# A latent-attention layer: element-wise work moved to GpSimd, one head group projected at a time

## The chip, the cores and the metric

The kernel runs on one core of one Trainium2 chip. The metric is the device time of one execution in microseconds (us). The engines are named as in the profile: PE is TensorE (matrix products; PEld are its weight loads), DVE is VectorE, ACT is ScalarE, POOL is GpSimd, and SP issues transfers. A line such as L922 is line 922 of the kernel before.

## The reference

The model is a trunk of two layers over 512 tokens of width 1024, in float32. Layer 0 mixes a state-space scan with gated linear attention, layer 1 is multi-head latent attention, and a SwiGLU block follows each. Only layer 1's attention is touched by the change:

```python
cq, ckv, k_rope = jnp.split(h @ w_dqkv, [MLA_Q_RANK, MLA_Q_RANK + MLA_KV_RANK], axis=-1)
q = (rms_norm(cq, q_lora_norm) @ w_uq).reshape(bsz, seqlen, H, MLA_NOPE + MLA_ROPE)
q_nope, q_rope = jnp.split(q, [MLA_NOPE], axis=-1)
kv = (rms_norm(ckv, kv_lora_norm) @ w_ukv).reshape(bsz, seqlen, H, MLA_NOPE + MLA_V)
k_nope, v = jnp.split(kv, [MLA_NOPE], axis=-1)
q_nope = rms_norm(q_nope, q_nope_norm)
q_rope = apply_rope(rms_norm(q_rope, q_rope_norm), cos[:, None, :], sin[:, None, :])
k_nope = rms_norm(k_nope, k_nope_norm)
k_rope = apply_rope(rms_norm(k_rope, k_rope_norm), cos, sin)
...
s = jnp.einsum('bqhd,bkhd->bhqk', qn, k_nope) + jnp.einsum('bqhr,bkr->bhqk', qr, k_rope)
p = jax.nn.softmax(jnp.where(mask, s * scale, -jnp.inf), axis=-1)
o = jnp.einsum('bhqk,bkhv->bqhv', p, v)
```

There are 16 heads; queries and keys have 64 plain and 32 rotary components, values 64, and the rotary key is shared by all heads. The low ranks are 384 for queries and 256 for keys and values.

## The kernel before, in words

Every large product is made in three passes of a rounded 32-bit type: each operand is split in a rounded part (hi) and the rest (lo), and hi x hi, hi x lo and lo x hi are added in one accumulator (mm3, L149 to L152). Weights come from memory through `weight` (L130): SP loads a raw tile (two buffers), ACT rounds it (L144), DVE takes the rest (L145); the rounded and the rest tiles have three buffers each. `weight` gives its instructions a priority some 90 instructions ahead, so weights are loaded as soon as a buffer comes free.

The kernel is written in program order, and a scheduler turns that order into one fixed queue per engine when the program is built: of the instructions that are ready it takes the one that stands earliest. So work that stands later in the code fills the gaps of work that stands earlier, when its inputs and buffers are there. On the chip each queue runs strictly in order.

The attention layer, in program order before the change:

1. The shared rotary key: 16 matmuls of 96 columns (L747, L748).
2. The low-rank queries (3 tiles) and keys/values (2 tiles) with their norms (L754 to L781).
3. The rotary key is turned, normalised and rotated, and copied into four key tiles kT, one by ACT (L818) and three by POOL (L820).
4. `project(0)` and `project(1)` (L957). A `project(g)` makes queries, keys and values of four heads for all 512 tokens: 36 matmuls of 384 columns and 24 of 512, evacuated by ACT (L838, L851, L852). Then squares on ACT (L856, L859), their sums on DVE (L857 to L860), an inverse root by three Newton steps on DVE (L862, L165 to L170), and on DVE the scale of the plain query part (L865), the scale of the rotary part (L868), its rotation in four steps (`rope`, L790 to L793) and the scale of the keys (L872). The query and key tiles have two buffers each, values three.
5. Eight times for a pair of heads: `prepare` of the pair after it, then `attend` of the pair itself. `prepare` transposes keys (L879) and queries (L892) on PE and evacuates them with ACT (L886, L894) and DVE (L888). `attend` goes through four blocks b of 128 queries with n = 128 (b + 1) keys. For each of the two heads j: the scores on PE (L911, two banks `sco`), scale, mask and maximum in one DVE step out of PSUM (L914), the exponent with its sum on ACT (L916); then for both heads the reciprocal (L919), the scale of the probabilities (L922, both on DVE), their transposes on PE (L925, two banks `ptr`) and the copy into `pt` by ACT (L929). The score tiles `sc` in SBUF have four buffers. At the end the values of both heads are gathered on PE (L934, bank `po`) and split into hi and lo (L126, L127).
6. `project(2)` stands behind attend 0 and `project(3)` behind attend 2 (`PROJ = (0, 2)`), the first half of the output projection (`o_round(0)`, L944) behind attend 4, the second half (`o_round(1)`) behind attend 7, and then the second SwiGLU block.

POOL is used in this layer for the mask and for the three copies of kT only.

Of the kernel before, what the change touches and what calls it, by code (L numbers as in the profile page):

```python
# [29 lines left out]
PROJ = (0, 2)  # L30
# [16 lines left out]
def kernel(ctx: ExitStack, tc: tile.TileContext, A, yT, stop=99):  # L47
# [15 lines left out]
    def acc():  # L63
        return pacc.tile([P, T], F32, tag="acc", name=nm("acc"))
# [65 lines left out]
    def weight(src, kc, m):  # L130

        with tc.high_priority(offset=AHEAD):
            return weight_now(src, kc, m)

    def weight_now(src, kc, m):
# [3 lines left out]
        return parts(r, kc, m)  # L139

    def parts(r, kc, m):
        hi = wp.tile([P, KD * P], F32R, tag="whi", name=nm("whi"))
        lo = wp.tile([P, KD * P], F32R, tag="wlo", name=nm("wlo"))
        S.copy(hi[:, :kc * m], r)  # L144
# [568 lines left out]
    with tc.tile_pool(name="mla", bufs=2) as mp, tc.tile_pool(name="mla1", bufs=1) as m1:  # L713
# [22 lines left out]
        wkr = wp.tile([P, KD * P], F32, tag="wraw", name="wkr", bufs=2)  # L736
        wkr = wkr[:, :KD * 32].rearrange("p (k m) -> p k m", k=KD)
        nc.sync.dma_start(wkr, A["w_kr"])
        w3 = wp.tile([P, KD * P], F32R, tag="whi", name="w3")
        w3 = w3[:, :KD * 96].rearrange("p (k j m) -> p k j m", k=KD, j=3)  # L740
        for j in range(2):
            S.copy(w3[:, :, j, :], wkr)
        V.tensor_tensor(w3[:, :, 2, :], wkr, w3[:, :, 0, :].bitcast(F32), ALU.subtract)
        ps = acc()
        for k, (xh, xl) in enumerate(xp):
            wk = w3[:, k].rearrange("p j m -> p (j m)")
            E.matmul(ps[:96], wk, xh, start=(k == 0), stop=False)  # L747
            E.matmul(ps[:96], wk, xl, start=False, stop=(k == KD - 1))  # L748
        krr = m1.tile([32, T], F32, name="krr")
        S.copy(krr, ps[64:96])  # L750
        V.tensor_tensor(krr, ps[:32], krr, ALU.add)

# [31 lines left out]
        def rope(dst, src, tab, shape):  # L784
# [9 lines left out]

        ps = aux()
# [26 lines left out]

        scale = 96 ** -0.5
        oparts = []

        def project(g):


            qs = mp.tile([P, 4, 4, 96], F32, tag="qs", name=nm("qs"))
            wqs = [weight(A["w_uq"][g, :, k0:k0 + n], n, 384) for k0, n in ((0, 2), (2, 1))]  # L830
            for i in range(4):
                ps = acc()
                for k in range(3):
                    lh, ll = lora["q"][k]
                    wh, wl = wqs[k // 2]
                    mm3(ps[:, :384], lh[:, i * P:(i + 1) * P], ll[:, i * P:(i + 1) * P],
                        wh[:, k % 2, :], wl[:, k % 2, :], k == 0, k == 2)
                S.activation(qs[:, i].rearrange("p h d -> p (h d)"), ps[:, :384], AF.Copy,  # L838
                             scale=cf["q"][:, i:i + 1])

            wkv = weight(A["w_ukv"][g], 2, 512)
            ks = mp.tile([P, 4, 4, 64], F32, tag="ks", name=nm("ks"))
            v = mp.tile([P, 4, 4, 64], F32, tag="v", name=nm("v"), bufs=3)
            for i in range(4):
                ps = acc()
                for k in range(2):
                    lh, ll = lora["kv"][k]
                    mm3(ps, lh[:, i * P:(i + 1) * P], ll[:, i * P:(i + 1) * P],
                        wkv[0][:, k, :], wkv[1][:, k, :], k == 0, k == 1)
                p3 = ps.rearrange("p (w h d) -> p w h d", w=2, h=4)  # L850
                S.activation(ks[:, i], p3[:, 0], AF.Copy, scale=cf["kv"][:, i:i + 1])  # L851
                S.activation(v[:, i], p3[:, 1], AF.Copy, scale=cf["kv"][:, i:i + 1])  # L852

            sq = mp.tile([P, 16, 96], F32, tag="sq", name=nm("sq"), bufs=1)
            st = mp.tile([P, 3, 16], F32, tag="st", name=nm("st"))
            S.activation(sq, qs.rearrange("p i h d -> p (i h) d"), AF.Square)  # L856
            V.tensor_reduce(st[:, 0], sq[:, :, 0:64], AX.X, ALU.add)  # L857
            V.tensor_reduce(st[:, 1], sq[:, :, 64:96], AX.X, ALU.add)
            S.activation(sq[:, :, 0:64], ks.rearrange("p i h d -> p (i h) d"), AF.Square)  # L859
            V.tensor_reduce(st[:, 2], sq[:, :, 0:64], AX.X, ALU.add)  # L860
            for j, n in enumerate((64, 32, 64)):
                V.tensor_scalar(st[:, j], st[:, j], 1.0 / n, EPS, ALU.mult, ALU.add)  # L862
            rf = rsqrt(mp, st, [P, 3, 16], "hr")
            q2 = qs.rearrange("p i h d -> p (i h) d")
            V.tensor_tensor(q2[:, :, 0:64], q2[:, :, 0:64],  # L865
                            rf[:, 0].unsqueeze(2).to_broadcast([P, 16, 64]), ALU.mult)
            rr = mp.tile([P, 16, 32], F32, tag="rr", name=nm("rr"), bufs=1)
            V.tensor_tensor(rr, q2[:, :, 64:96],  # L868
# [90 lines left out]
        for p in range(8):  # L959
# [5 lines left out]
            if p in PROJ:  # L965
                pr[2 + PROJ.index(p)] = project(2 + PROJ.index(p))
# [91 lines left out]
```

## Time and profile before

| what | value |
|---|---|
| time of three runs | 1370.97, 1372.99, 1373.26 us (median 1372.99) |
| the profiled execution's own time | 1371.09 us |
| its span, first to last instruction | 1368.9 us |
| granted TensorE clock | 0.999 |
| attention layer | from about 776 us (rotary key, L747) to about 989 us (last values, L934) |

Times in the profile are counted from the start of the span. A row of a group gives line, engine, operation, out<-in, count, then busy time and mean of one in ns, then the idle time of the engine just before these instructions and what ended it. A row of the order of time gives start and duration; several instructions can be merged in one row (x4). The rows by stretches give the busy time of each engine with the number of instructions in brackets, then the granted clock, the share of the transfer engines and GB/s. Matmul ends are modelled, so two matmuls in a row overlap in the rows.

### The profile page before, as it was taken

What the parts mean: (1) busy time and instruction counts of PE and PEld (TensorE: products, weight loads), DVE (VectorE), ACT (ScalarE), POOL (GpSimd) and SP (SyncE); (2) the same over time, 40 slices, a digit from 0 to 9 for tenths busy, and PEclk for the clock granted to TensorE, in tenths of its full rate; (3) what the DMA queues carried; (4) which work ended last, traced back from release to release, by engine and by line L of the source; (5) the groups of instructions that cost most, each with busy time, mean ns of one, the idle gap of its engine ahead of it and who ended that gap; (6) DMA issues with size and microseconds to landing.
All of it is one profiled execution on the core that took longest, in us unless ns stands there. A gap on an engine that the chain in (4) does not pass through costs nothing.

```text
span 1368.9 us, 16667 instructions
## 1 busy us (share of the span) xinstructions
PE 1344.9 (98%) x6506; PEld 1088.7 (80%) x6506; DVE 815.5 (60%) x1369; ACT 562.8 (41%) x941; POOL 7.8 (1%) x35
## 2 busy tenths in 40 slices
PE   8999999999999999999999999999999999999998
PEld 5788889788888888888888887666588888888887
DVE  7987976788867444444333469776594444443221
ACT  5584633544344322332232348775653322322121
POOL 0000000000000000000000000000000000000000
PEclk9999999999999999999999999999999999999999
DMA  5342232222233333223333321111033223323331
GB/s 177 109 141 91 77 95 78 78 77 62 79 93 105 93 94 106 92 92 99 90 100 100 101 68 56 39 47 62 1 98 103 93 93 102 98 93 108 111 103 63
DMA packets 36781, 122.22 MB, mean 89 GB/s; under 512 B 4768, under 2 KB 5792, under 8 KB 36704
## 3 DMA queue, kind: packets, MB, share of 16 engines
q1 hardware_dynamic: 35888, 120.72, 28.1%
q8 instruction: 51, 0.84, 0.2%
q10 hardware_dynamic: 816, 0.46, 0.1%
q14 instruction: 26, 0.21, 0.0%
HBM read 119.03 MB, written 2.13 MB: 89 GB/s over the span
## 4 chain that ended last, share of the span: by engine, by line
PE 90%; DVE 5%; ACT 3%; issue 1%; DMA 1%; SPq 0%; ACTq 0%
PE acc L150 27%; PE acc L151 27%; PE acc L152 27%; PE sco L911 2%; PE ptr L925 1%; PE po L934 1%; DVE wlo L145 1%; PE a L447 1%; PE a L625 0%; PE a L433 0%; PE a L614 0%; PE a L451 0%; ACT whi L144 0%; PE a L627 0%; DVE gm L534 0%
## 5 line engine op out<-in xcount | busy, mean ns | idle before, releaser
L150 PE MATMUL acc<-xh,whi 128*128 128x512 f32 x1144 | 449.1, 393 | 5.2 <-DVE dp L322 2.5
L144 ACT CAST whi<-wraw 128x1024 fp32r<-128x1024 f32 (+2 forms) x221 | 225.8, 1022 | 554.0 <-PE acc L151 436.9
L151 PE MATMUL acc<-xl,whi 128*128 128x512 f32 x1144 | 448.7, 392 | 0.0
L152 PE MATMUL acc<-xh,wlo 128*128 128x512 f32 x1144 | 448.7, 392 | 0.0
L145 DVE TENSOR_TENSOR wlo<-wraw,whi 128x1024 fp32r<-128x1024 f32 (+2 forms) x221 | 261.9, 1185 | 163.2 <-ACT whi L144 163.1
L150 PEld LDWEIGHTS acc<-xh,whi 128*128 128x128 f32 x1144 | 214.9, 188 | 51.2 <-ACT cvt L366 2.8
L152 PEld LDWEIGHTS acc<-xh,wlo 128*128 128x128 f32 x1144 | 215.1, 188 | 44.8 <-DVE wlo L145 0.6
L151 PEld LDWEIGHTS acc<-xl,whi 128*128 128x128 f32 x1144 | 215.1, 188 | 44.5 <-issue 1.4
L152 PE MATMUL acc<-fhh,wlo 128*128 128x512 f32 x288 | 112.0, 389 | 0.0
L150 PE MATMUL acc<-fhh,whi 128*128 128x512 f32 x288 | 112.0, 389 | 0.0
L151 PE MATMUL acc<-fhl,whi 128*128 128x512 f32 x288 | 112.0, 389 | 0.0
L683 DVE TENSOR_TENSOR fu<-acc,R 128x512 f32<-128x512 f32 x44 | 30.4, 691 | 136.2 <-PE acc L152 136.2
L680 DVE TENSOR_TENSOR fg<-acc,R 128x512 f32<-128x512 f32 x44 | 30.4, 691 | 89.0 <-PE acc L152 88.9
L152 PEld LDWEIGHTS acc<-fhh,wlo 128*128 128x128 f32 x288 | 54.1, 188 | 11.3
L151 PEld LDWEIGHTS acc<-fhl,whi 128*128 128x128 f32 x288 | 54.1, 188 | 11.3
L150 PEld LDWEIGHTS acc<-fhh,whi 128*128 128x128 f32 x288 | 54.1, 188 | 11.1
L151 PE MATMUL acc<-mxl,whi 128*128 128x512 f32 x128 | 49.9, 391 | 0.0
L150 PE MATMUL acc<-mxh,whi 128*128 128x512 f32 x128 | 49.8, 391 | 0.0
L152 PE MATMUL acc<-mxh,wlo 128*128 128x512 f32 x128 | 49.7, 390 | 0.0
L911 PE MATMUL sco<-kT,qT 96*128 96x128 f32 (+3 forms) x128 | 42.8, 445 | 1.5 <-DVE mx L914 1.3
L914 DVE CUSTOM_DVE_ANT_0 sc<-sco,am 128x128 f32<-128x128 f32 (+3 forms) x64 | 30.7, 487 | 13.6 <-PE sco L911 11.5
L916 ACT ACTIVATE sc<-sc,mx 128x128 f32<-128x128 f32 (+3 forms) x64 | 35.7, 561 | 7.3 <-DVE mx L914 6.8
(329 smaller groups left out, 1584.8 us busy)
## 6 DMA issues: line engine op xcount, KB each, us to landing
wraw<-in_w_gate_dram SPq DMA_DIRECT2D x44, 512.0 KB, 3.5
wraw<-in_w_up_dram SPq DMA_DIRECT2D x44, 512.0 KB, 3.5
wraw<-in_w_down_dram SPq DMA_DIRECT2D x32, 512.0 KB, 3.6
wraw<-in_w_out_dram SPq DMA_DIRECT2D x16, 512.0 KB, 3.6
wraw<-in_w_xbc_dram SPq DMA_DIRECT2D x12, 512.0 KB, 3.6
wraw<-in_w_down_dram SPq DMA_DIRECT2D x16, 384.0 KB, 3.1
wraw<-in_w_z_dram SPq DMA_DIRECT2D x8, 512.0 KB, 3.5
wraw<-in_w_v_dram SPq DMA_DIRECT2D x8, 512.0 KB, 3.5
```

Of the source, the lines that this page charges most:

```text
L144: S.copy(hi[:, :kc * m], r)
L145: V.tensor_tensor(lo[:, :kc * m], r, hi.bitcast(F32)[:, :kc * m], ALU.subtract)
L150: E.matmul(out, ah, bh, start=first, stop=False)
L151: E.matmul(out, ah, bl, start=False, stop=False)
L152: E.matmul(out, al, bh, start=False, stop=last)
L447: E.matmul(pd[64 * h:64 * h + 64, c * P:(c + 1) * P], xdt[:, c, h, :], mt[:, h, c, :], start=True, stop=True)
L680: V.tensor_tensor(g, pg, R, ALU.mult)
L683: V.tensor_tensor(u, pu, R, ALU.mult)
L911: E.matmul(ps[:, :n], qts[j][:, b * P:(b + 1) * P], kts[j][:, :n], start=True, stop=True)
L914: V.tensor_tensor_reduce(sc[:, :n], ps[:, :n], am[:, T - n:], -scale, 3e38, ALU.add, ALU.min, mx[:, j:j + 1])
L916: S.activation(sc[:, :n], sc[:, :n], AF.Exp, bias=mx[:, j:j + 1], scale=-1.0, accum_out=sm[:, j:j + 1])
L925: E.transpose(ps[:, kb * P:(kb + 1) * P], sc[:, kb * P:(kb + 1) * P], ident)
```

## The change: what it does

- `weight` and `parts` take an optional engine for the rounding; the weights of `project` and `o_round` are rounded by POOL in place of ACT (11 in the stretch of the attends, 20 in all).
- In `project`, POOL does the two scales of the queries, the rotation of the queries (`rope` takes an engine) and the scale of the keys: seven instructions for each of four groups, before on DVE.
- In `attend`, POOL scales the probabilities, before on DVE (64 instructions). The copy of the transposed probabilities is made by DVE for the second head of a pair and stays on ACT for the first.
- The order in the code: `project(0)` stands ahead of the rotary key's matmuls, which before stood ahead of the low-rank products. `project(1)`, `project(2)` and `project(3)` stand behind attends 0, 1 and 3 (`PROJ = (0, 1, 3)`).

```diff
-PROJ = (0, 2)
+PROJ = (0, 1, 3)
...
-    def parts(r, kc, m):
+    def parts(r, kc, m, copy=None):
...
-        S.copy(hi[:, :kc * m], r)
+        (copy or S.copy)(hi[:, :kc * m], r)
...
-        def rope(dst, src, tab, shape):
+        def rope(dst, src, tab, shape, V=V):
...
-            wqs = [weight(A["w_uq"][g, :, k0:k0 + n], n, 384) for k0, n in ((0, 2), (2, 1))]
+            wqs = [weight(A["w_uq"][g, :, k0:k0 + n], n, 384, G.tensor_copy) for k0, n in ((0, 2), (2, 1))]
...
-            wkv = weight(A["w_ukv"][g], 2, 512)
+            wkv = weight(A["w_ukv"][g], 2, 512, G.tensor_copy)
...
-            V.tensor_tensor(q2[:, :, 0:64], q2[:, :, 0:64],
+            G.tensor_tensor(q2[:, :, 0:64], q2[:, :, 0:64],
                             rf[:, 0].unsqueeze(2).to_broadcast([P, 16, 64]), ALU.mult)
...
-            V.tensor_tensor(rr, q2[:, :, 64:96],
+            G.tensor_tensor(rr, q2[:, :, 64:96],
                             rf[:, 1].unsqueeze(2).to_broadcast([P, 16, 32]), ALU.mult)
-            rope(qs[:, :, :, 64:96], rr.rearrange("p (i h) d -> p i h d", i=4), tabs[0], [P, 4, 4, 32])
+            rope(qs[:, :, :, 64:96], rr.rearrange("p (i h) d -> p i h d", i=4), tabs[0], [P, 4, 4, 32], G)
             k2 = ks.rearrange("p i h d -> p (i h) d")
-            V.tensor_tensor(k2, k2, rf[:, 2].unsqueeze(2).to_broadcast([P, 16, 64]), ALU.mult)
+            G.tensor_tensor(k2, k2, rf[:, 2].unsqueeze(2).to_broadcast([P, 16, 64]), ALU.mult)
...
-                    V.tensor_scalar(sc[:, :n], sc[:, :n], sm[:, j:j + 1], None, ALU.mult)
+                    G.tensor_scalar(sc[:, :n], sc[:, :n], sm[:, j:j + 1], 1.0, ALU.mult, ALU.mult)
...
-                    last = S.copy(dst, ps[:, :n].rearrange("p (k q) -> p k q", q=P))
+                    last = (V.tensor_copy if j else S.copy)(dst, ps[:, :n].rearrange("p (k q) -> p k q", q=P))
...
-                w = weight(A["w_o"][r, m2], 4, 256)
+                w = weight(A["w_o"][r, m2], 4, 256, G.tensor_copy)
...
-        pr = {0: project(0), 1: project(1)}
+        pr = {0: first}
...
-                pr[2 + PROJ.index(p)] = project(2 + PROJ.index(p))
+                pr[1 + PROJ.index(p)] = project(1 + PROJ.index(p))
```

In the code, `first = project(0)` now stands right behind the low-rank products, and the block that loads, multiplies and adds the rotary key (L736 to L751) follows it.

More of the change, by code (lines that the diff above doesn't have):

```diff
@@ L732 @@
                         pattern=[[-1, P]], channel_multiplier=1)
[L736 to L751, printed above, removed]
         lora, cf = {}, {}
```

105 lines of the change are left out of this document (61 added, 44 removed).

## The prediction

> **What bounds the kernel now.** I read the page first, then the busy time of each engine by stretches of the attention stage, then what every idle piece waited for, then the order of time on VectorE (DVE) and TensorE (PE) in the two worst places. The page:
>
> ```profile
> span 1368.9 us, 16667 instructions
> PE 1344.9 (98%) x6506; PEld 1088.7 (80%) x6506; DVE 815.5 (60%) x1369; ACT 562.8 (41%) x941; POOL 7.8 (1%) x35
> ```
>
> PE sets the time, POOL is empty. The whole kernel can't gain more than what PE loses, so the question is where PE loses time and whether the moved work causes it. By stretches (columns: PE, PEld, DVE, ACT, POOL busy, clock, DMA share, GB/s), with the last row the whole of the attends:
>
> ```profile
> 822.00:836.00 14.00, 13.49 (x71) 11.65 (x69) 13.31 (x35) 11.24 (x21) 1.75 (x3) 1.00 0.07 20
> 836.00:923.00 87.00, 78.80 (x418) 55.28 (x420) 70.50 (x214) 67.71 (x163) 0.00 (x0) 1.00 0.16 50
> 950.00:965.00 15.00, 13.88 (x77) 9.05 (x78) 11.77 (x45) 12.81 (x38) 0.00 (x0) 1.00 0.13 36
> 965.00:977.00 12.00, 11.87 (x64) 6.93 (x62) 8.32 (x33) 9.00 (x28) 0.00 (x0) 1.00 0.01 2
> 836.00:989.00 153.00, 142.91 (x751) 97.88 (x751) 110.25 (x332) 106.70 (x266) 0.00 (x0) 1.00 0.13 43
> ```
>
> From 836 to 989 us PE idles 153.00 - 142.91 = 10.1 us, and 8.2 us of that (87.00 - 78.80) lie before 923 us, where the normalisation of the projected heads shares DVE with the softmax. One attend without that, 965 to 977 us, idles 0.13 us. So the loss belongs to the projections' company, not to the attend as such. The clock is 1.00 throughout and the transfers use 13%, so neither counts. The idle time understates the loss: a matmul of 512 columns lasts 0.39 us but the next starts 0.23 us after it (the rows at 775.96 and 776.19 below), so each stop also costs some 0.16 us of overlap. Who makes PE stop, in the same stretch (total us, times, longest):
>
> ```profile
> PEld sco L911 <- DVE mx L914: 9.8, 23, 0.7
> PEld acc L150 <- ACT qT L894: 4.0, 2, 2.2
> PEld ptr L925 <- ACT pt L929: 3.0, 8, 0.5
> PEld ptr L925 <- DVE sc L922: 2.0, 4, 1.1
> ```
>
> These are 37 stops. DVE frees the score banks late (L914), ACT frees the accumulators and the transpose banks late (L894, L929). One of the worst places, on DVE and on PE:
>
> ```profile
> 870.57 1.22 DVE L865 TENSOR_TENSOR qs<-qs,hry 128x1024 f32<-128x1024 f32 x1
> ...
> 874.11 0.68 DVE L792 TENSOR_TENSOR qs<-rr,csq 128x512 f32<-128x512 f32 x1
> 874.71 0.55 DVE L914 CUSTOM_DVE_ANT_0 sc<-sco,am 128x384 f32<-128x384 f32 x1
> ...
> 870.70 1.12 PE L911 MATMUL sco<-kT,qT 96*128 96x512 f32 x2
> 873.17 0.45 PE L150 MATMUL acc<-whi,lh 128*128 128x384 f32 x1 [1.35 <-ACT qT L894]
> ```
>
> From 870.57 to 874.71 DVE does nothing but scale and rotate one group's queries and keys; the next score step waits 4.1 us behind it. The change moves just these instructions.
>
> **The change part by part.** Durations of what moves, from the groups of DVE and of ACT in 836 to 989 us (busy us, mean ns):
>
> ```profile
> L914 DVE CUSTOM_DVE_ANT_0 sc<-sco,am 128x128 f32<-128x128 f32 (+3 forms) x64 | 30.7, 487 | 13.6 <-PE sco L911 11.5 <-PE ptr L925 1.7
> L922 DVE TENSOR_SCALAR sc<-sc,sm 128x128 f32<-128x128 f32 (+3 forms) x64 | 22.2, 383 | 0.7
> L865 DVE TENSOR_TENSOR qs<-qs,hry 128x1024 f32<-128x1024 f32 x3 | 3.7, 1220 | 0.0
> L872 DVE TENSOR_TENSOR ks<-ks,hry 128x1024 f32<-128x1024 f32 x3 | 3.7, 1217 | 0.0
> L793 DVE TENSOR_TENSOR qs<-qs,rt 128x512 f32<-128x512 f32 x4 | 2.7, 682 | 0.0
> L868 DVE TENSOR_TENSOR rr<-qs,hry 128x512 f32<-128x512 f32 x3 | 2.0, 682 | 0.0
> L792 DVE TENSOR_TENSOR qs<-rr,csq 128x512 f32<-128x512 f32 x3 | 2.0, 681 | 0.0
> L790 DVE TENSOR_TENSOR rt<-rr,csq 128x256 f32<-128x256 f32 x3 | 1.2, 416 | 0.0
> L791 DVE TENSOR_TENSOR rt<-rr,csq 128x256 f32<-128x256 f32 x3 | 1.2, 416 | 0.0
> L929 ACT COPY pt<-ptr 128x128 f32<-128x128 f32 (+3 forms) x64 | 24.3, 429 | 11.0 <-PE ptr L925 11.0
> L144 ACT CAST whi<-wraw 128x1024 fp32r<-128x1024 f32 (+2 forms) x11 | 10.8, 985 | 10.7 <-PE acc L151 10.7
> ```
>
> DVE loses the scale of the probabilities, 22.2 us, and per projection 1.22 + 1.22 + 3 x 0.68 + 2 x 0.42 = 5.3 us, three of them in this stretch: 16 us. It gains half of the copies out of the transpose banks: 32 at the price of L914, which reads PSUM in the same four widths, 32 x 0.487 = 15.6 us. Net 110.3 - 22.2 - 16 + 15.6 = 88 us of work. ACT loses half of L929 (12.2 us) and the roundings (10.8): 106.7 - 23 = 84 us. PE has the same work as before.
>
> POOL's price has only two rows like it:
>
> ```profile
> L820 POOL COPY kT<-kT 32x512 f32<-32x512 f32 x3 | 1.8, 618 | 49.0 <-ACT kT L818 49.0
> L110 POOL CAST ones_r<-ones 128x128 fp32r<-128x128 f32 x1 | 0.3, 289 | 0.0
> ```
>
> A straight line through them is 0.18 us + 0.86 ns an element. The scale at 128 to 512 columns is then 0.29, 0.40, 0.51, 0.62 us, or 3.6 us for an attend (DVE: 8 x 0.383 = 3.1); its upper bound is two passes of a copy, 7.3 us. A projection's seven instructions have two inputs: 4.8 us as single passes (2 x 1.06 + 3 x 0.62 + 2 x 0.40), 9.6 us as two passes each; I take 9.6, since two inputs are read. The roundings of 1024, 768 and 384 columns are 1.06, 0.84, 0.51 us, as on ACT (0.985 on average). With eight attends, three projections and 11 roundings POOL carries 29 + 29 + 11 = 69 us, 98 at the upper bound, of some 145 us: it keeps up on average, but its queue is in order.
>
> What is new on the path: DVE's reciprocal now hands over to POOL. The one hand-over to POOL in this stage, in the order of time on ACT and on POOL:
>
> ```profile
> 825.40 0.57 ACT L818 COPY kT<-sco 32x512 f32<-32x512 f32 x1
> 826.12 1.75 POOL L820 COPY kT<-kT 32x512 f32<-32x512 f32 x3 [49.00 <-ACT kT L818]
> ```
>
> It took 826.12 - 825.97 = 0.15 us. With 2 x 0.07 us for the slower scale that is some 0.3 us in each of 32 blocks, 9 us on the attends' own chains. The other block and the next head fill PE meanwhile (0.13 us idle in an attend that already runs such chains); without that cover it is all 9 us. I take a quarter, 2 us. Bounds 0 and 9.
>
> A second cost is in the one place where POOL and DVE already work together, POOL's copies of kT from 826.12 to 827.87 us:
>
> ```profile
> 826.87 0.48 DVE L165 TENSOR_SCALAR hri<-st 128x48 int32<-128x48 int32 x1
> 827.39 0.52 DVE L166 TENSOR_SCALAR hry<-hri 128x48 int32<-128x48 int32 x1
> ...
> L165 DVE TENSOR_SCALAR hri<-st 128x48 int32<-128x48 int32 x3 | 0.6, 185 | 0.0
> ```
>
> The same instruction takes 0.185 us without POOL: 0.3 us lost each time. A projection has five of this kind (L862 three times, L165, L166), so up to 1.7 us each, 5 us in the stretch; DVE then holds 93 of some 145 us and still has room. At the lower bound, where POOL is idle just then, it is nothing. The two-input instructions that stay on DVE (nine of the Newton steps and three L145 in a projection) have no row beside a working POOL; if each lost 0.3 us too, that is 3.6 us more a projection, 11 us in all, and DVE is back at 104. The Trainium skill (Advanced Engine Details and Errata, VectorE Performance Modes) says that DVE's second SBUF port is shared with POOL and that two-port DVE instructions and POOL block each other; the same page (Miscellaneous Facts) adds DVE instructions with two SBUF inputs. The trace agrees for L165 (0.48 against 0.185 us). By the page the 11 us would be counted, and the gain below would be about 4 us smaller.
>
> Order of the projections and the rotary key: its 16 matmuls (0.23 us apart, so 3.7 us) move behind project(0):
>
> ```profile
> 775.96 0.39 PE L747 MATMUL acc<-xh,w 128*96 128x512 f32 x1
> 776.19 0.40 PE L748 MATMUL acc<-xl,w 128*96 128x512 f32 x1
> ...
> 822.79 0.33 PE L152 MATMUL acc<-whi,ll 128*128 128x384 f32 x1
> 835.09 0.60 PE L879 MATMUL acc<-ident,ks 128*128 128x128 f32 x4
> ```
>
> So project(0) ends at about 822.8 - 3.7 = 819.1 us, and until the first transposes of keys PE has the rotary key (3.7) and project(1) (12.3, from 822.79 to 835.09), which comes later in the code but needs nothing of the attends: cover to 835.1. The chain behind project(0) now runs through POOL; before, it took from 822.8 until 835.1. Now it is 12.3 + 9.6 - 5.3 = 16.6 us long, less some 2 us that DVE gave to the rotary key and a rounding remainder inside it: 833.7 to 835.7. POOL must also fit the three copies of kT (1.75) behind it. I put the start of the attends at no change; bounds 2 us earlier, 4 later. If the cover by project(1) fails (its weights late), it costs up to 12 us; its transfers are issued by SP as before and the row says 7% of DMA there. In the attends the fill is what it was: the third projection still needs the first group's query buffer back.
>
> Sum. In 836 to 923 us I let the idle time fall to a third, since the blocks of 4.1 us leave DVE and ACT drops by a fifth: -5.5 us. Of the 37 stops I let 25 go, 25 x 0.16 = -4 us; 950 to 965 us gives 0.5. New chains +2. Total -8 us, with bounds of -15 (all of the 8.2 and 1.1 us and 37 x 0.16 = 5.9) and of the rivals below. The profiled execution took 1371.1 us, its span and 2.2 us around it, and lies 1.9 us under the median of the runs. Against the median: 1373.0 - 8 = 1365 us.
>
> **The rivals.** (1) PE nearly packed: all 15 us come back, 1358 us. For it: 965 to 977 us shows that an attend can run at 0.13 us of idle time. Against it: the stops that ACT's and DVE's ordinary hand-overs make are small and many (0.7 us at most for L914), and these remain. (2) The freed work was not on the path: the bank waits stay because the score, exponent and transpose steps set them, and PE merely waits for POOL instead of DVE: 1371 to 1375 us. For it: DVE and ACT are at 72% and 70% in the stretch, not full. Against it: the 4.1 us at 870.57. (3) Slower: POOL's one queue. A projection's seven instructions stand ahead of an attend's scale; on DVE that block was 4.1 us, on POOL it is up to 9.6, so the transposes wait 5.5 us longer in each of three places, 16 us, and the gain of 8 is overrun: 1373 - 8 + 16 = 1381 us. It decides where PE has no projection matmuls left to fill with (12.3 us a projection, from 822.79 to 835.09). If the scale also costs two passes, the last three attends, which have no projection to fill with, add up to 3 x 4.2 us; with the block half covered that is 1373 - 8 + 8 + 13 = 1386 us. For it: PE's order is fixed when the program is built. Against it: transposes waited for the scale for only 2.0 us in all, though DVE's block existed three times. The Trainium skill (GPSIMD Engine Reference, When to use GPSIMD) advises VectorE for elementwise work, POOL being about twice as slow with two inputs; no run here shows it yet, and by it the projection would be 2 x 5.3 = 10.6 us on POOL, near the bound that I took.
>
> **How the numbers follow.** The forecast (-8, own range 1359 to 1369 us) 0.48; (1) 0.18; (2) 0.13; (3) 0.21. What lies within 0.2%, 2.7 us, can't be told from no change. Faster: 0.48 + 0.18 = 0.66; same 0.13; slower 0.21. The range goes from 1355, three under (1), to 1377, which takes in (2) and the half of (3) in which the block is partly filled.
>
> **What would show it.** Right: the row of 836 to 989 us shorter by about 8 us with PE idle under 5 us; DVE at some 60% and L914 no longer waiting 4 us behind L792; POOL near 70 us busy, 0.6 us for the widest scale and about 2.1 us for L865. The port: DVE's small steps at 0.3 to 0.5 us when POOL runs. Wrong: transposes (L925) that wait for POOL for more than 10 us in all, a gap before the first attend of over 4 us, or seven POOL instructions of a projection that together pass 12 us.

## The result and the profile after

The changed kernel takes 1423.43 us (median; 1421.80 to 1424.21), the kernel before 1373.12 us in the same comparison: a ratio of 1.0368, 95% interval 1.035 to 1.0386. It is slower by 50 us, where 1365 was forecast and 1381 to 1386 was the worst case that the prediction priced.

The page of the changed kernel: its span, the engines, and from the 40 slices PE, POOL and the granted clock.

```profile
span 1421.6 us, 16740 instructions
PE 1366.0 (96%) x6506; PEld 1101.8 (78%) x6506; DVE 801.5 (56%) x1309; ACT 539.4 (38%) x889; POOL 93.4 (7%) x147
PE   8999999999999999999999967788999999999998
POOL 0000000000000000000000033334310000000000
PEclk9999999999999999999999978889999999999999
```

ACT lost the work that was planned (562.8 to 539.4 us). DVE lost 14 us (815.5 to 801.5), less than the 22 us that the prediction has for the stage of the attends alone. POOL went from 7.8 to 93.4 us. The holes in PE and the dips of the clock lie where POOL works.

The stretches of the attention stage (columns as in the prediction: PE, PEld, DVE, ACT, POOL busy, clock, DMA share, GB/s). The first and third row have the same borders as two rows shown of before.

```profile
822.00:836.00 14.00, 4.71 (x23) 3.04 (x21) 12.36 (x26) 2.29 (x4) 7.03 (x7) 0.75 0.14 43
830.00:840.00 10.00, 0.90 (x3) 0.50 (x3) 9.55 (x17) 0.00 (x0) 8.63 (x7) 0.50 0.07 20
836.00:989.00 153.00, 121.89 (x558) 86.61 (x558) 70.67 (x206) 72.63 (x167) 60.13 (x77) 0.84 0.09 32
880.00:890.00 10.00, 2.93 (x12) 1.34 (x10) 3.43 (x12) 2.63 (x6) 8.65 (x9) 0.67 0.00 1
920.00:930.00 10.00, 3.64 (x16) 2.32 (x16) 2.22 (x8) 3.16 (x8) 9.92 (x10) 0.72 0.00 0
970.00:980.00 10.00, 5.88 (x24) 4.19 (x24) 2.02 (x5) 1.66 (x5) 9.66 (x11) 0.78 0.00 0
```

There are four holes, one for each group of heads: at 830, 880, 920 and 970 us POOL is busy for nearly nine tenths of the time or more, and PE for 0.9, 2.9, 3.6 and 5.9 us of ten. Before, the stretch of 14 us from 822 to 836 us had 13.49 us of PE work in it; now it has 4.71. The clock is at 0.50 in the first hole and below 0.80 in the others.

What PE waited for from 822 to 1040 us (us in total, times, longest), first its matmuls, then its weight loads:

```profile
PE acc L881 <- POOL ks L827: 15.0, 3, 6.8
PE ptr L927 <- POOL sc L924: 13.3, 12, 4.1
PE sco L866 <- DVE kro L776: 4.7, 1, 4.7
PEld ptr L927 <- POOL sc L924: 28.8, 45, 4.5
```

L881 and L927 are the transposes of the keys and of the probabilities, L827 and L924 POOL's scale of the keys and of the probabilities. A wait of a matmul and of its weight load overlap, so the two lists are not added. Before, the worst of such waits of the matmuls was:

```profile
PE acc L150 <- ACT qT L894: 3.0, 2, 1.6
```

The first hole, in the order of time on PE, POOL and DVE:

```profile
828.05 0.43 PE L851 MATMUL sco<-ident,krr 32*128 32x32 f32 x4 [2.46 <-DVE krr L848]
830.48 1.90 POOL L820 TENSOR_TENSOR qs<-qs,hry 128x1024 f32<-128x1024 f32 x1 [3.38 <-DVE krm L859]
830.66 1.75 DVE L166 TENSOR_SCALAR lry<-lri 128x4 int32<-128x4 int32 x1
832.34 1.05 POOL L823 TENSOR_TENSOR rr<-qs,hry 128x512 f32<-128x512 f32 x1
832.44 0.96 DVE L168 TENSOR_TENSOR lrt<-lry 128x4 f32<-128x4 f32 x1
833.35 1.90 POOL L827 TENSOR_TENSOR ks<-ks,hry 128x1024 f32<-128x1024 f32 x1
833.44 1.82 DVE L169 SCALAR_TENSOR_TENSOR lrt<-krm,lrt 128x4 f32<-128x4 f32 x1
835.30 0.90 PE L881 MATMUL acc<-ident,ks 128*128 128x128 f32 x3 [6.83 <-POOL ks L827]
839.24 0.16 DVE L169 SCALAR_TENSOR_TENSOR lrt<-krm,lrt 128x4 f32<-128x4 f32 x1
840.90 1.03 PE L866 MATMUL sco<-ident,kro 128*32 128x128 f32 x4 [4.69 <-DVE kro L776]
846.62 0.44 PE L150 MATMUL acc<-whi,lh 128*128 128x384 f32 x1
```

Two things are to be seen. PE has nothing to do although project(1) could run: its first matmul (the last row) starts at 846.62 us, behind all transposes of the first group. And DVE's steps for the rotary key, on four numbers a partition, take 1.75, 0.96 and 1.82 us; each ends when the POOL instruction beside it ends (830.48 + 1.90 = 832.38 and 830.66 + 1.75 = 832.41; 833.35 + 1.90 and 833.44 + 1.82 are 835.25 and 835.26). Where POOL rests, the same step takes 0.16 us (L169 at 839.24). PE waits 4.69 us for this chain, at 840.90.

The three other holes, on PE:

```profile
887.32 1.12 PE L881 MATMUL acc<-ident,ks 128*128 128x128 f32 x4 [4.84 <-POOL ks L827]
924.90 1.12 PE L881 MATMUL acc<-ident,ks 128*128 128x128 f32 x4 [3.36 <-POOL ks L827]
976.58 0.90 PE L927 MATMUL ptr<-ident,sc 128*128 128x128 f32 x3 [4.07 <-POOL sc L924]
```

In the second and third, the key transposes of groups 1 and 2 wait for their normalisation, as in the first. In the fourth, the transposes of the probabilities wait for POOL's scale, which stands behind six of the seven instructions of group 3.

Worked out from the matmuls and the clock's intervals in the traces, for 815 to 1100 us: PE idles 41.6 us, before 10.7; and the clock is at half for 54.6 us, before never. PE had work in 33.4 us of these, and half of that, 16.7 us, is lost: a matmul of 512 columns takes 0.78 us at half clock (981.52 us) and 0.39 right behind it (982.51). The idle time grew by 41.6 - 10.7 = 30.9 us, and 30.9 + 16.7 = 47.6 us of the 52.7 by which the two profiled spans differ.

### The profile page after: what moved, and what is told of

Same layout as the page of the kernel before. It is cut to its first block, busy times and chain, and to the rows that moved or that the text cites. A ratio compares the mean times of both kernels' runs of the same rounds, so it can differ in the third digit from the quotient of the medians.

```text
span 1421.6 us, 16740 instructions
## 1 busy us (share of the span) xinstructions
PE 1366.0 (96%) x6506; PEld 1101.8 (78%) x6506; DVE 801.5 (56%) x1309; ACT 539.4 (38%) x889; POOL 93.4 (7%) x147
## 4 chain that ended last, share of the span: by engine, by line
PE 87%; DVE 5%; ACT 2%; POOL 2%; DMA 2%; issue 2%; SPq 0%; POOLq 0%; DVEq 0%; ACTq 0%
PE acc L152 26%; PE acc L151 26%; PE acc L150 25%; PE sco L913 2%; PE ptr L927 2%; PE po L936 1%; DVE wlo L145 1%; PE acc L894 1%; PE a L447 1%; DVE sc L916 1%; POOL sc L924 1%; PE a L625 0%; PE a L433 0%; PE a L614 0%; POOL qs L820 0%
## 5 line engine op out<-in xcount | busy, mean ns | idle before, releaser
L144 ACT CAST whi<-wraw 128x1024 fp32r<-128x1024 f32 (+1 forms) x201 | 207.9, 1035 | 532.0 <-PE acc L151 420.3
L150 PEld LDWEIGHTS acc<-fhh,whi 128*128 128x128 f32 x288 | 54.1, 188 | 11.3
L151 PEld LDWEIGHTS acc<-fhl,whi 128*128 128x128 f32 x288 | 54.1, 188 | 11.2
L913 PE MATMUL sco<-kT,qT 96*128 96x128 f32 (+3 forms) x128 | 47.0, 484 | 4.0 <-DVE mx L916 4.0
L927 PE MATMUL ptr<-ident,sc 128*128 128x128 f32 x160 | 33.2, 325 | 13.7 <-POOL sc L924 13.3
L927 PEld LDWEIGHTS ptr<-ident,sc 128*128 128x128 f32 x160 | 21.1, 161 | 32.1 <-POOL sc L924 28.8
```

The lines of the kernel that those rows point to most:

```text
L144: (copy or S.copy)(hi[:, :kc * m], r)
L150: E.matmul(out, ah, bh, start=first, stop=False)
L151: E.matmul(out, ah, bl, start=False, stop=False)
L913: E.matmul(ps[:, :n], qts[j][:, b * P:(b + 1) * P], kts[j][:, :n], start=True, stop=True)
L927: E.transpose(ps[:, kb * P:(kb + 1) * P], sc[:, kb * P:(kb + 1) * P], ident)
```

## The experiments

Four theories. **Order**: one group at a time leaves a group's normalisation uncovered. **POOL's queue**: the scale of the probabilities stands behind a projection's seven instructions. **Port**: DVE and POOL hold each other up. **Clock**: idle time makes PE slow afterwards. All line numbers of the experiments are those of the changed kernel, up to some twenty lines more or less.

### The order back, POOL's work kept

```diff
-PROJ = (0, 1, 3)
+PROJ = (0, 2)
...
-        pr = {0: first}
+        pr = {0: project(0), 1: project(1)}
...
-                pr[1 + PROJ.index(p)] = project(1 + PROJ.index(p))
+                pr[2 + PROJ.index(p)] = project(2 + PROJ.index(p))
```

The projection of the rotary key stands ahead of project(0) again, too.

> The changed kernel with the order of before: project(1) stands ahead of the first prepare again, projections 2 and 3 behind attends 0 and 2, and the rotary key ahead of project(0). All of POOL's work stays on POOL. Theory 'order' (each group's normalisation is exposed because its transposes take the accumulator banks, in program order, ahead of the next projection's matmuls): most of the 50 us returns, 1365 to 1385 us, PE idle in 836 to 989 us no more than some 12 us, clock 1.00 there. Theory 'POOL's queue' (transposes wait for POOL's scale, whatever the order): 1400 us or more, and PE still waits over 25 us in all for L924 and L827. Theory 'port' (VectorE is slowed whenever POOL works): between them, 1385 to 1400 us.

Measured: 1400.17 us, 1.0203 (1.0188 to 1.0219). Only 23 us came back, less than the theory of the order expected; the theory of the queue fits the number, and PE still waits:

```profile
PEld ptr L927 <- POOL sc L924: 29.8, 42, 4.8
```

How one such wait comes about, in the order of time on POOL and PE:

```profile
852.98 1.90 POOL L837 TENSOR_TENSOR qs<-qs,hry 128x1024 f32<-128x1024 f32 x1
...
855.23 0.17 DVE L921 RECIPROCAL sm<-sm 128x2 f32<-128x2 f32 x1 [0.83 <-ACT sc L918]
...
860.32 0.48 POOL L924 TENSOR_SCALAR sc<-sc,sm 128x256 f32<-128x256 f32 x1
860.76 1.28 POOL L793 TENSOR_TENSOR qs<-qs,rt 128x512 f32<-128x512 f32 x1
860.85 0.69 PE L927 MATMUL ptr<-ident,sc 128*128 128x128 f32 x2 [4.34 <-POOL sc L924]
...
895.14 0.90 PE L927 MATMUL ptr<-ident,sc 128*128 128x128 f32 x3 [4.28 <-POOL sc L924]
939.75 0.55 PE L927 MATMUL ptr<-ident,sc 128*128 128x128 f32 x3 [4.36 <-POOL sc L924]
```

Six of project(1)'s seven instructions run from 852.98 to 860.34. The scale of the second block, whose reciprocal was there by 855.40, starts at 860.32, and the transposes follow. The last two rows are the same wait behind the seven of groups 2 and 3. This is the prediction's third rival, as it was described. PE idles 26.4 us from 815 to 1100 us, 15.7 more than before, of which these three waits make 13.0; the clock adds 9.0.

### The order alone, POOL empty

The changed kernel with all that went to POOL, and the copies, on the engines of before; of the seven instructions the first is shown:

```diff
-            G.tensor_tensor(q2[:, :, 0:64], q2[:, :, 0:64],
+            V.tensor_tensor(q2[:, :, 0:64], q2[:, :, 0:64],
...
-                    G.tensor_scalar(sc[:, :n], sc[:, :n], sm[:, j:j + 1], 1.0, ALU.mult, ALU.mult)
+                    V.tensor_scalar(sc[:, :n], sc[:, :n], sm[:, j:j + 1], None, ALU.mult)
...
-                    last = (V.tensor_copy if j else S.copy)(dst, ps[:, :n].rearrange("p (k q) -> p k q", q=P))
+                    last = S.copy(dst, ps[:, :n].rearrange("p (k q) -> p k q", q=P))
```

> Only the order of the changed kernel (one group at a time, the rotary key behind project(0)); the scale, the seven instructions of a projection, the roundings and the copies are on the engines of before, so POOL is as empty as before. Theory 'order': well above before, 1395 to 1415 us, with PE waiting at the front (830 to 846 us) and ahead of each group's first attend. Theory 'POOL's queue' or 'port': within 5 us of before, 1370 to 1378 us.

Measured: 1395.99 us, 1.0174 (1.0159 to 1.019): 23 us lost with POOL as empty as before, as the theory of the order had it. With the run above, 23 + 27 = 50 us: the two halves of the loss add up.

### The seven instructions back on VectorE

All seven, of which the first is shown:

```diff
-            G.tensor_tensor(q2[:, :, 0:64], q2[:, :, 0:64],
+            V.tensor_tensor(q2[:, :, 0:64], q2[:, :, 0:64],
...
```

> The changed kernel with the seven scale-and-rotate instructions of a projection back on VectorE; scale of the probabilities and roundings stay on POOL, the order stays new. Theory 'order': the chain behind a projection is shorter by 9 minus 5 us and VectorE's small steps are not blocked by it, four times, so some 15 to 25 us come back: 1398 to 1410 us. Theory 'POOL's queue': the scales no longer stand behind a block of 8.8 us, so nearly all comes back: 1370 to 1385 us. Theory 'port': likewise nearly all of what the chain blocks comes back, the slow Newton steps (1.75 us instead of 0.17) go, 1385 to 1400 us.

Measured: 1403.38 us, 1.0229 (1.0212 to 1.0246). 20 of the 50 us come back with these 28 instructions, within what the order theory expected and just above the port's range. As the order theory itself counts a part of the port in its range, the run tells the two apart badly; it does rule out that the scale behind the block was nearly all. Against the order-only kernel it is 7 us slower: in this order the scale, the copies and the roundings cost 7 us, and the seven instructions on top of them 20.

### Another bank for prepare's transposes, in the changed kernel

```diff
         def prepare(g, hp, qs, ks, v):
-            ps = acc()
+            ps = aux("po")
...
-                ps = acc()
+                ps = aux("po")
```

> The changed kernel with one edit: the transposes of prepare take the bank of the attend's output (po) instead of the ring of three accumulators, so that the next projection's matmuls need not stand behind them. Theory 'order': project(1)'s matmuls fill the front and project(2)'s and project(3)'s fill the waits of prepare(1) and (2): 20 to 45 us less than the changed kernel, 1378 to 1403 us, the first attend no later than 838 us. Theory 'POOL's queue': the scales still stand behind the block on POOL: 1415 us or more.

Measured: 1398.25 us, 1.0187 (1.0171 to 1.0202): 25 us back with one edit, as much as the whole order back. Transposes of the keys now wait for POOL for 4.1 us in all instead of 15.0. The first attend's scores start at 844.26 us, not by 838 as expected and only 2.0 us earlier than in the changed kernel: PE now waits 5.4 us for the rotary key, whose steps on VectorE are held up beside POOL as above.

### The moves one at a time, in the order of before

Scale of the probabilities on POOL, half of the copies on VectorE:

```diff
-                    V.tensor_scalar(sc[:, :n], sc[:, :n], sm[:, j:j + 1], None, ALU.mult)
+                    G.tensor_scalar(sc[:, :n], sc[:, :n], sm[:, j:j + 1], 1.0, ALU.mult, ALU.mult)
...
-                    last = S.copy(dst, ps[:, :n].rearrange("p (k q) -> p k q", q=P))
+                    last = (V.tensor_copy if j else S.copy)(dst, ps[:, :n].rearrange("p (k q) -> p k q", q=P))
```

> The kernel before with one pair moved: the scale of the probabilities goes to POOL, half of the copies out of the transpose banks to VectorE. Theory 'block' (the scale is late only where a projection's seven instructions stand ahead of it in POOL's queue): without them on POOL nothing waits long, 1368 to 1376 us, transposes wait for POOL under 8 us in all. Theory 'hop' (each hand-over to POOL and its slower scale cost something in each of 32 blocks): 1380 us or more, with waits for L924 spread over all 32 blocks.

Measured: 1383.57 us, 1.0082 (1.0065 to 1.0099). The hop theory fits: 46 weight loads wait, none longer than 1.7 us. But the hop has company; the same 64 instructions take 535 ns on average in the changed kernel and 630 here, 6 us more in all, where a projection's seven run on VectorE beside them:

```profile
PEld ptr L927 <- POOL sc L924: 22.9, 46, 1.7
L924 POOL TENSOR_SCALAR sc<-sc,sm 128x128 f32<-128x128 f32 (+3 forms) x64 | 39.4, 630 | 127.2 <-DVE sm L921 102.4 <-DVE hry L170 17.0 <-PE acc L152 2.9
847.58 3.24 POOL L924 TENSOR_SCALAR sc<-sc,sm 128x128 f32<-128x128 f32 x2 [17.02 <-DVE hry L170]
847.60 1.23 DVE L837 TENSOR_TENSOR qs<-qs,hry 128x1024 f32<-128x1024 f32 x1
```

The third row: two scales of 128 columns take 3.24 us, because VectorE starts an instruction with two inputs 0.02 us later (the fourth row). So the hold-up works against POOL too.

Only the seven instructions of a projection on POOL, of which the first is shown:

```diff
-            V.tensor_tensor(q2[:, :, 0:64], q2[:, :, 0:64],
+            G.tensor_tensor(q2[:, :, 0:64], q2[:, :, 0:64],
...
```

> The kernel before with only a projection's seven scale-and-rotate instructions on POOL; the scale of the probabilities stays on VectorE, so no softmax step can stand behind the block. Theory 'block': the loss of the order-back kernel (27 us) needs both in one queue, so here most is gone, 1370 to 1378 us, what is left being the first attend, whose keys come 4 to 6 us later. Theory 'port' (VectorE's own instructions are held up while POOL runs two-input ones): VectorE's softmax steps beside the blocks are several times slower, 1380 to 1390 us.

Measured: 1381.46 us, 1.0067 (1.0052 to 1.0082), the port's range. PE's matmuls also wait 4.1 us for the longer chain of the first group, so the 8 us are not the port's alone. VectorE's scale costs 31.4 us instead of 22.2, while its step out of PSUM costs what it did (487 ns):

```profile
L924 DVE TENSOR_SCALAR sc<-sc,sm 128x128 f32<-128x128 f32 (+3 forms) x64 | 31.4, 527 | 0.9
L916 DVE CUSTOM_DVE_ANT_0 sc<-sco,am 128x128 f32<-128x128 f32 (+3 forms) x64 | 30.7, 487 | 15.8 <-PE sco L913 14.9 <-PE ptr L927 0.8
```

Only the roundings of the weights of the projections and of w_o on POOL, of which one is shown:

```diff
-            wkv = weight(A["w_ukv"][g], 2, 512)
+            wkv = weight(A["w_ukv"][g], 2, 512, G.tensor_copy)
...
```

> The kernel before with only the roundings of the weights of projections and of w_o on POOL. Theory 'block': ScalarE gets 10 to 15 us free and POOL is empty otherwise: 1368 to 1374 us. Theory 'port': a copy on POOL also holds up VectorE for up to 1 us, 19 roundings, of which a half fall on busy stretches: 1374 to 1382 us.

Measured: 1374.54 us, 1.0009 (0.9999 to 1.0019): nothing that can be told from no change. The moves cost 10, 8 and 1 us one at a time and 27 all together, so some 7 us arise only in company. That is not the price of the shared queue, because the hold-ups change too. Added up over the traces, as what each instruction took beyond its usual length where POOL is empty, VectorE loses 13 us in the second run and POOL 6 in the first; with all moves together and the order back it is 5 and 1, since the scale and the two-input steps then lie on one engine.

### The port by itself

The kernel before, with the seven instructions done a second time on POOL, on the tile of the squares, whose sums are taken by then; two of the seven are shown, the others have the shapes of the rest:

```diff
+            s1, s2 = sq[:, :, 0:64], sq[:, :, 64:96]
...
+            G.tensor_tensor(s1, s1, rf[:, 0].unsqueeze(2).to_broadcast([P, 16, 64]), ALU.mult)
+            G.tensor_tensor(s2, s2, rf[:, 1].unsqueeze(2).to_broadcast([P, 16, 32]), ALU.mult)
...
             V.tensor_tensor(q2[:, :, 0:64], q2[:, :, 0:64],
```

> The kernel before, with a second copy of a projection's seven scale-and-rotate instructions on POOL, on scratch data (the squares, once they are summed): the same shapes and the same time as in the kernel with only these moved, but the real ones stay on VectorE and nothing waits for POOL. Theory 'port' (an instruction of VectorE that runs beside one of POOL is held up until POOL's ends, and the other way round): VectorE's scale of the probabilities beside them takes over 0.8 us on average instead of 0.38, the kernel is 5 to 15 us slower, 1378 to 1388 us. Theory 'waits only' (the loss comes from PE's waits for POOL's results): no change, 1371 to 1376 us.

Measured: 1404.14 us, 1.0227 (1.0211 to 1.0243), twice the upper end of what the port's theory expected. From this kernel's trace, VectorE and POOL in the order of time, and two groups:

```profile
830.93 2.39 DVE L852 TENSOR_TENSOR rr<-qs,hry 128x512 f32<-128x512 f32 x1
832.74 1.49 POOL L842 TENSOR_TENSOR sq<-sq,hry 128x512 f32<-128x512 f32 x1
L841 POOL TENSOR_TENSOR sq<-sq,hry 128x1024 f32<-128x1024 f32 x4 | 13.6, 3388 | 71.1 <-DVE hry L170 35.8 <-ACT pt L943 35.3
L852 DVE TENSOR_TENSOR rr<-qs,hry 128x512 f32<-128x512 f32 x4 | 7.0, 1751 | 0.0
```

Instructions of both engines lengthen to the time of both: 1.75 us instead of 0.68 on VectorE, 3.39 instead of 1.90 on POOL. It is as if one port served them in turn. VectorE's seven become a block of over 10 us. Four of VectorE's scales ran beside them and took 1.1 us on average.

The time of this run is not the port's price, however. The tile of the squares has one buffer, so the next group's squares on ACT wait for POOL's last instruction, twice, and PE waits for the evacuations behind them in ACT's queue:

```profile
842.44 1.48 ACT L828 ACTIVATE sq<-qs 128x1536 f32<-128x1536 f32 x1 [9.45 <-POOL sq L847]
844.71 1.94 PE L906 MATMUL acc<-ident,qs 128*96 128x128 f32 x8 [8.62 <-ACT v L824]
```

So something does wait for POOL, against the expectation's premise. The lengths show that the engines hold each other up; how much of the 31 us is due to that was not separated.

### Useless work for PE

```diff
         def prepare(g, hp, qs, ks, v):
 
+            if hp == 0:
+                fill = aux("ptr")
+                w0 = lora["kv"][0][0]
+                for _ in range(16 if g else 24):
+                    E.matmul(fill, w0[:, 0:P], w0, start=True, stop=True)
```

> The order-only kernel (POOL empty, 1396 us) with useless matmuls for PE to do while it would wait: 24 of 512 columns ahead of the first group's prepare and 16 ahead of each of the other three, 72 x 0.23 = 16.6 us of added work, their result never read. Theory 'clock' (each stretch in which PE idles is followed by a stretch at half clock, and that costs 13.6 us of the order-only kernel's 23): the half clock goes or shrinks, and the kernel gets faster with more work, 1381 to 1391 us. Theory 'idle only' (what is lost is the idle time itself): the fill lies inside the waits at best, 1396 to 1400 us, and what does not fit comes on top, up to 1412.

Measured: 1403.31 us, 1.0218 (1.0204 to 1.0232), 7 us above the order-only kernel. The expectation of the clock theory fell, and the number lies in the range of 'idle only'. The clock theory's price was wrong: 13.6 us is half of the 27.3 us at half clock, but PE idled in part of those; the work in them loses 9.0 us. The balance now holds: 16.6 us of work added, idle time 25.0 to 16.5 us, loss by the clock 9.0 to 7.5, so 16.6 - 8.5 - 1.5 = 6.6 us. The fill did cut the time at half clock (27.3 to 17.1 us), but not enough to pay.

### The two parts of the order

One group at a time, with the rotary key ahead of project(0) as before (from the order-only kernel), and the rotary key behind project(0) on the kernel before:

```diff
+        wkr = wp.tile([P, KD * P], F32, tag="wraw", name="wkr", bufs=2)
...
+        V.tensor_tensor(krr, ps[:32], krr, ALU.add)
...
         lora, cf = {}, {}
```

In the second kernel, project(0) is called ahead of the rotary key:

```diff
-        pr = {0: project(0), 1: project(1)}
+        pr = {0: first, 1: project(1)}
```

> The order-only kernel with the rotary key back ahead of project(0): what is left is one group at a time. Theory 'order by the ring' (prepare's transposes stand ahead of the next projection in the ring of accumulators): nearly the whole loss stays, 1388 to 1398 us, since the rotary key was only 3.7 us of cover. Theory 'rotary key' (its chain from PE over ScalarE and VectorE back to PE, now late, holds the first attend): 8 to 15 us come back, 1380 to 1388 us.

> The kernel before with the rotary key's projection between project(0) and project(1), and nothing else moved. Theory 'ring': project(1) still stands ahead of prepare in the ring, so the chain behind project(0) stays covered, and the rotary key's 3.7 us only change places: 1369 to 1376 us. Theory 'rotary key' (its chain over ScalarE and VectorE ends later than the first attend needs it): 1378 to 1388 us.

Measured: 1401.87 us, 1.021 (1.0196 to 1.0224) for the first, and 1374.32 us, 1.0002 (0.9992 to 1.0011) for the second. One group at a time costs 28 us by itself; the late rotary key gives 6 of it back, and alone does nothing. That it does so as cover for PE was not tested. The second is what the ring theory expected, the first lies a few us above it.

### The bank and the order, POOL empty

The same edit of the bank, on the kernel before and on the order-only kernel:

```diff
-            ps = acc()
+            ps = aux("po")
...
-                ps = acc()
+                ps = aux("po")
```

> The kernel before with one edit: the transposes of prepare take the bank of the attend's output (po) instead of the ring of three accumulators; nothing is moved between engines. Theory 'order' (the ring, handed out in program order, makes projections wait for prepare): the 10 us of idle time and the waits of L150 for ACT's qT shrink, 1362 to 1370 us. Against it: before has the projections ahead in the ring anyway, so within 3 us of before, or slower by the output bank's wait (two buffers), 1373 to 1380 us.

> The order-only kernel (1396 us) with prepare's transposes in the bank of the attend's output instead of the ring of accumulators; POOL empty. The same edit made the kernel before slower by 7 us (1380 us). Theory 'ring' (the order loses time only because prepare's transposes hold the ring ahead of the next projection's matmuls): the order then costs nothing on top of the 7 us, 1376 to 1385 us. Theory 'order itself' (each group's chain is exposed whatever the bank, since one projection of 12 us cannot cover it): 1392 us or more.

Measured: on before 1380.39 us, 1.0056 (1.0039 to 1.0072), so the gain that the theory of the order expected there did not come; on the order-only kernel 1365.63 us, 0.9941 (0.9923 to 0.9958). The output's bank is a single buffer, not two as the first expectation has it, and that serialises the transposes: on before they wait there up to 3.8 us. But with the new order the edit gives 30 us, more than its theory expected, and the result beats both kernels, by 7.8 us against before. The stage of that kernel, and how its PE passes the first group's chain:

```profile
822.00:836.00 14.00, 14.00 (x78) 12.22 (x77) 13.77 (x40) 9.79 (x17) 0.00 (x0) 1.00 0.26 80
836.00:923.00 87.00, 84.80 (x448) 60.89 (x447) 71.91 (x226) 71.24 (x177) 1.71 (x3) 0.96 0.13 44
...
822.28 0.34 PE L150 MATMUL acc<-whi,lh 128*128 128x384 f32 x1
...
829.79 0.39 PE L150 MATMUL acc<-whi,lh 128*128 128x512 f32 x1
830.02 0.60 PE L881 MATMUL po<-ident,ks 128*128 128x128 f32 x4
830.37 0.48 PE L151 MATMUL acc<-wlo,lh 128*128 128x512 f32 x1
```

project(1)'s matmuls start at 822.28 us, 24 us earlier than in the changed kernel, and the first transposes slip in between two of them at 830.02. PE idles nowhere in the 14 us from 822, and 2.2 us up to 923, where before it was 8.2.

The four corners: new order with the ring 1396, with its own bank 1366; the same with POOL's work 1423 and 1398. POOL's work costs 27 us with the ring and 33 without it.

### POOL only where no projection runs beside it

```diff
+            late = 2 * g + hp >= 4
...
+                    if late:
+                        G.tensor_scalar(sc[:, :n], sc[:, :n], sm[:, j:j + 1], 1.0, ALU.mult, ALU.mult)
+                    else:
+                        V.tensor_scalar(sc[:, :n], sc[:, :n], sm[:, j:j + 1], None, ALU.mult)
...
-                    last = S.copy(dst, ps[:, :n].rearrange("p (k q) -> p k q", q=P))
+                    last = (V.tensor_copy if late and j else S.copy)(dst, ps[:, :n].rearrange("p (k q) -> p k q", q=P))
```

> The kernel before with the scale on POOL and half of the copies on VectorE for the last four attends alone, where the seven instructions of a projection no longer run beside them for three of the four. Theory 'block and port' (POOL's scale only hurts beside a projection's work): 1368 to 1374 us, the last three attends as fast as in the changed kernel (11.2 us from one value step to the next). Theory 'hop' (every hand-over costs): 1374 to 1380 us.

Measured: 1374.13 us, 1.0008 (0.9999 to 1.0017). No change: the last four attends neither lose by the hop nor gain by the freed engines. The last values follow each other after 11.3 and 11.2 us, as in the changed kernel; before, it was 12.2 and 10.8. So the hop costs little where no projection's work runs beside it, and DVE's and ACT's relief is worth nothing where PE already runs through.

## Why the prediction was wrong, step by step

**"Cover to 835.1" failed, and with it the order.** The prediction held that project(1) comes later in the code but needs nothing of the attends, and so fills PE. It named its weights as the one way in which this could fail. It overlooked the accumulators: three banks, handed out in the order of the code. With one group at a time, prepare asks for them first, and its transposes wait for the normalisation while they hold the ring. The weights were there by 829.3 us; the matmuls came at 846.62. (Before, project(1) began at 822.44 us and not at 822.79, as the prediction reads; that changes nothing.) Other banks for the transposes gave back 25 to 30 us, the order alone cost 23. The bound of 12 us for the failed cover was for one place; the trace of the changed kernel has three, of 6.83, 4.84 and 3.36 us. In the order-only kernel, PE idles 25.0 - 10.7 = 14.3 us more than before and loses 9.0 us by the clock, which is the 23. "In the attends the fill is what it was" failed in the same way: before, project(g+1) always stood a group ahead in the ring.

**The port was mis-sized, and taken for mere load.** 0.3 us for each one-input instruction, five in a projection, was read from one short meeting with a copy on POOL. The runs show that an instruction is held until the other engine's ends: 1.75 us for 0.16. It also hits instructions that the sum left untouched: two-input ones (the 11 us that stood only as an upper bound), VectorE's scale (9 us in the run with the seven alone), and POOL's own (6 us in the run with the scale alone). The prediction's sum took them at nothing, against the rule that it cited from the Trainium skill (Advanced Engine Details and Errata, Miscellaneous Facts); the trace agrees with that rule, 1.75 us against 0.68 for L852 in the run of the port by itself. In the changed kernel VectorE loses some 10 us this way and POOL nothing. That amount lies between the 5 us counted and the upper bound; but 7 of the 10 us fall on the rotary key's chain, for which PE waits, where the prediction saw only busy time of an engine with room.

**The hop was 2 us, bounds 0 and 9.** Scale and copies alone cost 10.4 us. That is above both bounds, but some 6 us of POOL's time in it are the port, which the changed kernel does not have there; how much of the rest is the hop alone was not separated.

**POOL's one queue stood in no term of the sum.** It was the third rival, given 21%, with 16 us for three places. With the order back, these three waits are 4.34, 4.28 and 4.36 us, 13.0 in all, nearly as priced. They are most of the 15.7 us by which PE idles longer in that kernel, and with the clock's 9.0 us that makes 24.7 of its 27. The rival came out too small (1381 us) because it still took off the gain of 8 us and knew nothing of the clock and of the order.

**Prices that held.** The seven instructions: 9.6 us forecast, 8.8 measured (2 x 1.90 + 1.05 + 2 x 0.73 + 1.26 + 1.27). Rows of POOL:

```profile
L820 POOL TENSOR_TENSOR qs<-qs,hry 128x1024 f32<-128x1024 f32 x4 | 7.6, 1901 | 5.3 <-DVE krm L859 3.4 <-DVE hry L170 1.9
L776 POOL TENSOR_TENSOR qs<-qs,rt 128x512 f32<-128x512 f32 x4 | 5.1, 1266 | 0.1
L924 POOL TENSOR_SCALAR sc<-sc,sm 128x128 f32<-128x128 f32 (+3 forms) x64 | 33.4, 535 | 65.4 <-DVE sm L921 59.3 <-PE sco L913 4.6 <-PE acc L152 1.4
```

The scale took 535 ns on average against 455 forecast (the mean of its four widths); none of these rows is held up by VectorE in the changed kernel. Of the three signs of a wrong forecast that it named, two came: transposes that wait for POOL over 10 us, and gaps before the first attend of over 4 us (6.83 and 4.69 us). The third, the seven over 12 us, did not.

**The clock was said not to count.** That was so before, at 1.00 throughout. In the traces it follows the idle time (the last section), and it added 16.7 us to 30.9; no range of the prediction had it.

**The gain of 8 us** shows in no run that moves work to POOL. The best kernel shows that most of the 8.2 us of idle time ahead of 923 us can be had: it takes back 6.0 of them by the order and the bank, and leaves DVE and ACT with what they had. Its gain of 7.8 us is not fully accounted for: from 815 to 1100 us the idle time falls by 5.0 us, and 6.8 us at half clock take 3.4 of that away again. Why the single output bank hurts on the order of before and not on the new one was not separated further.

## What to carry to other kernels

Ask of every tile in a ring who gets it first in the order of the code: a consumer that waits on a long chain must not stand ahead of independent work in the same ring. Don't take POOL for a free engine beside a busy VectorE: compare the lengths of both engines' instructions with those that they have alone. A second copy of the work shows this as well, but its time is no price (31 us here, where the real move cost 8), least of all when its tile is needed elsewhere. Count PE's idle time with what the clock adds.

## What the runs showed of the hardware

**VectorE and POOL in turn.** Held up beside POOL: VectorE's scale from SBUF to SBUF (0.48 to as much as 1.94 us for 512 columns), its two-input steps (0.16 to 1.8 us on four numbers a partition), and POOL's scale beside two-input ones (0.37 to 1.85 us for 128 columns). Not held up in the run with the seven alone: the score step out of PSUM (290 ns alone and 288 beside POOL for 128 columns, 688 and 684 for 512), sums along a row (1.22 us both ways) and the reciprocal of two numbers (0.16 us).

**PE's clock.** Over the traces of all 16 kernels, from some 20 to 1085 us, cut at the 3.41 us grid on which the clock changes: a window at full clock in which PE idled 2 us or more was followed by one at half clock in 37 of 37 cases, with 1.6 to 2.0 us in 24 of 33, with 1.2 to 1.6 us in 3 of 34, and with less in none of 4768. The idle time need not be one gap: in a window of the kernel with the late rotary key it was 1.6 us with no gap over 0.5. The Trainium skill (TensorE: Matmul & The Clock Gate, Why this matters for your kernels) advises no gaps over some 3 us; here about 1.7 us in a window, half of it, were mostly enough.
